# Scan products in a fixed order on TensorE, each step in one run between whole projection tiles, and tanh for the convolution's gate

## The chip, the core and the metric

The kernel runs on one core of a Trainium2 chip. The metric is the time of one execution on the device in microseconds (us); the time of the kernel before is the median of three runs. A core has TensorE (matrix products; PE in the profile, with its weight loads as PEld), VectorE (DVE), ScalarE (ACT), GpSimd (POOL), SyncE (SP, which here issues the DMAs) and 16 DMA engines. PSUM is the memory into which TensorE writes and from which VectorE and ScalarE read. Each engine works through its own list of instructions in order and waits on semaphores where a result of another is needed.

## The reference, cut to what matters

One layer of a hybrid block over 512 latent tokens of width 1024, with 256 context tokens ahead whose final scan state starts the scan of the latent ones. One input projection feeds a convolution branch (A) and a bidirectional scan (B), in 8 groups of 4 heads; then come gates, an output projection and an MLP. All is float32.

```python
h = modulate(rmsnorm(x, norm1_w), mod[0], mod[1]); proj = h @ w_in
# A: the gated input and a depthwise convolution of width 31 along grid rows of 64
glu = proj[..., COL_GLU:COL_GATE]
u = glu[..., :CONV_DIM] * jax.nn.sigmoid(glu[..., CONV_DIM:])
u = dwconv(u.reshape(rows, 64, CONV_DIM), conv_dw_w, conv_dw_b)
u_conv = silu(layernorm(u)) @ w_conv_out + b_conv_out
# B: for x, B and C a centred convolution of width 5 and SiLU, then, in each direction, by chunks of 128:
cum = jnp.cumsum(dt * a)
cb = jnp.einsum('bcqgn,bckgn->bcgqk', cs_, bs)
y_diag = jnp.einsum('bcgrqk,bckgrp->bcqgrp', cb[:, :, :, None] * decay, xdt)
states = jnp.einsum('bcqgn,bcqgr,bcqgrp->bcgrpn', bs, decay_to_end, xdt)
h_in = scan over the chunks of  h * chunk_decay + states      # from the context's final state
y_off = jnp.einsum('bcqgn,bcgrpn,bcqgr->bcqgrp', cs_, h_in, jnp.exp(cum))
y = y_f + flip(y_b) + ssm_d * xs
y = rmsnorm(y * silu(z), ssm_norm_w);  u_ssd = y @ w_ssm_out
x = x + mod[2] * ((g_conv * u_conv + g_ssd * u_ssd) @ w_o)      # g: sigmoid gates from proj
x = x + mod[5] * sq_relu_mlp(modulate(rmsnorm(x, norm2_w), ...))
```

## The kernel before

Channels lie on the 128 partitions and tokens in the free dimension. The input projection is cut into tiles of 128 output columns. For each, `load_w` (L99 to L107) brings the 512 KB weight tile by a DMA of SP's, ScalarE casts it to its high part `whi` (L105) and VectorE takes the difference, the low part `wlo` (L106). `gemm` (L109 to L116) then makes the product in three passes, `whi` by the input's high part (L114), `whi` by its low part (L115) and `wlo` by the high part (L116): 8 slices by 3, so 24 matmuls of 512 columns for a whole tile. The tiles of B and of the two x tiles (X0, X1) have 24 more of 256 columns for the context. Two weight tiles are held at a time (`raw`, `whi` and `wlo` have two buffers each), and the products go to three PSUM buffers `ps`.

A group's projection (`proj`, L415) gives six tiles: B, C, X0, X1 (`xbc`, L377) and the gates Z0, Z1. Those of B, C and x leave PSUM by `taps5` (L367 to L375), the convolution of width 5: one ScalarE instruction (L370) and four of VectorE (L374), then SiLU on ScalarE (L384). Those of Z leave by a SiLU (L430).

A group's scan (`ssd`, L437) has these steps, named here as in the change:

- **c**: B by C for the four chunks (`cps`, L442), masked on VectorE (`cbm`, L447), and B turned by TensorE (`bps`, L454) and copied by ScalarE (`Bk`, L455).
- **x**: x turned by TensorE (`xps`, L465), multiplied by VectorE with what reaches the chunk's end (`xw`, L470) and copied by ScalarE (`xt`, L477).
- **s**: the states' products (`sps`, L485) and their running sum on VectorE (`hst`, L491 to L498).
- **y0, y1**: the outputs of two heads each. A DMA (L507) brings the running sums of one head and direction (`cfb`). ScalarE makes the decays (four Relu, L510, and one Exp, L512), VectorE multiplies by `cbm` (L513), ScalarE (L517) and VectorE (L520) mix the two directions, and GpSimd or VectorE multiplies C by the decays (`Cd`, L523). TensorE adds 16 products of the states and `Cd` (L536) and 8 of x and the mix (L532) in one PSUM tile `yps`. VectorE adds D·x (L540), multiplies by Z (L541), and a DMA writes the tile (L542).

Branch A runs beside the scan. `glu` (L551) makes two projection tiles, takes the sigmoid of the one on ScalarE (L557) and multiplies with the other on VectorE (L562). `taps` (L565) is the convolution of width 31: one ScalarE instruction (L569) and 30 of VectorE (L575) for a tile of 128 channels.

The main loop (L585 to L593) traces `ssd(g)`, then `proj(g + 1)`, then, for the first five groups, a tile of branch A. The order on each engine is not that of the text: a scheduler picks the ready instruction of the best priority, and `later(n)` moves priorities (weights 300 earlier, evictions of projections 400 earlier, `glu` 90 later, `taps` 650 later). The order is fixed when the kernel is built. So matmuls of the scan stand among those of the projection tiles, wherever the scheduler took their inputs to be ready. After the scan come the other three tiles of branch A, the gates, branch A's LayerNorm, the two branch projections, the output projection and the MLP.

Of the kernel before, what the change touches and what calls it, by code (L numbers as in the profile page):

```python
# [26 lines left out]
# columns of the packed per-channel vectors  # L27
# [8 lines left out]
# order of the input projection's 128-column tiles  # L36
# [6 lines left out]
# the groups beside which the first tiles of the convolution module run  # L43
GLU_AT = (0, 1, 2, 3, 4)
# [12 lines left out]
def build(tc, xT, ctxT, cond, crow, wada1, wada2, vecs, hv, cst, w_in, w_co, w_so, w_o, w_1, w_2, outT):  # L57
    nc = tc.nc
    with ExitStack() as es:
# [49 lines left out]
        def gemm(ps, w, rhs, start=True, stop=True, t0=0, t1=None, k0=0, k1=KT):  # L109
# [3 lines left out]
            for k in range(k0, k1):  # L113
                nc.tensor.matmul(ps, lhsT=whi[:, k, :], rhs=rhi[:, k, t0:t1], start=start and k == 0, stop=False)  # L114
                nc.tensor.matmul(ps, lhsT=whi[:, k, :], rhs=rlo[:, k, t0:t1], start=False, stop=False)  # L115
                nc.tensor.matmul(ps, lhsT=wlo[:, k, :], rhs=rhi[:, k, t0:t1], start=False, stop=stop and k == KT - 1)  # L116
# [13 lines left out]
        def rsqrt_mean(ps, n, cnt, r=None):  # L130
            """1/sqrt(sum/cnt + EPS) of a sum broadcast over the partitions"""
# [18 lines left out]
        def rsqrt_rows(parts, n, cnt, pool, out=None):  # L150
            """the same of the sum of several tiles, found token by token and then spread over the partitions"""
# [40 lines left out]
        with tc.tile_pool(name="st", bufs=1) as st:  # L192
# [31 lines left out]
            # products of nothing: the tensor engine's clock halves when it idles  # L224
# [83 lines left out]
            # softplus: max(v, 0) + log1p(u), u = exp(-|v|), log1p(u) = 2 atanh(u / (2 + u))  # L308
# [13 lines left out]
            # running sums within the chunks and within the context, backward ones from the end  # L322
# [22 lines left out]
            # step s: chunk s forward, chunk 3 - s backward  # L345
# [41 lines left out]
        def xbc_first():  # L387
            """the first group's, all of x's part before ctx's"""
# [162 lines left out]
        def glu(t, pool, tag):  # L551
# [4 lines left out]
            with later(-EVICT_GLU):  # L556
                nc.scalar.activation(sg, pb, AF.Sigmoid)  # L557
# [319 lines left out]
```

## Time and profile before

| | us |
|---|---|
| three runs | 1263.03, 1266.08, 1270.63 |
| median | 1266.08 |
| profiled execution, span | 1264.2 |
| VectorE's first multiplication of step x (L470) of groups 0, 1, 2, 6, 7 | 104.1, 162.8, 235.2, 520.6, 577.3 |
| end of the scan's outputs | 621.6 |

The profile is of one execution; its times count from the start of its span. The median lies 1.9 us above the span. Step x is used as a mark below: "from x of group 1 to x of group 2" is the stretch between VectorE's first multiplication of step x (L470) in the one and in the other. A group row gives an instruction's line, engine, operation and tiles, how many there are, their busy time, the mean in ns of one, and then the engine's idle time just before them with what ended it. A timeline row gives start, duration and instruction, and `x8` where eight in a row were put together. The scan's float32 products are two records each in the trace; its turnings by TensorE (`bps`, `xps`) and the projections' matmuls (fp32r) are one.

### The profile page before, as it was taken

What the parts mean: (1) busy time and instruction counts of PE and PEld (TensorE: products, weight loads), DVE (VectorE), ACT (ScalarE), POOL (GpSimd) and SP (SyncE); (2) the same over time, 40 slices, a digit from 0 to 9 for tenths busy, and PEclk for the clock granted to TensorE, in tenths of its full rate; (3) what the DMA queues carried; (4) which work ended last, traced back from release to release, by engine and by line L of the source; (5) the groups of instructions that cost most, each with busy time, mean ns of one, the idle gap of its engine ahead of it and who ended that gap; (6) DMA issues with size and microseconds to landing.
All of it is one profiled execution on the core that took longest, in us unless ns stands there. A gap on an engine that the chain in (4) does not pass through costs nothing.

```text
span 1264.2 us, 17493 instructions
## 1 busy us (share of the span) xinstructions
PE 1220.7 (97%) x6665; PEld 995.6 (79%) x6665; DVE 953.7 (75%) x1567; ACT 667.4 (53%) x1124; POOL 108.9 (9%) x74
## 2 busy tenths in 40 slices
PE   6998999999999899999999999999999999999997
PEld 3786778777787778787888877778998888888886
DVE  6797689999999999998999798885843343443444
ACT  4557888686776748868453452134431331331442
POOL 0001222121020302124000000000000000000000
PEclk8999999999999999999999999999999999999999
DMA  9424363343342424333363357964222333233332
GB/s 363 142 67 133 137 198 128 120 146 106 121 159 93 158 83 147 112 134 117 109 193 126 119 188 258 305 196 153 62 65 86 100 100 92 92 100 101 96 104 67
DMA packets 56260, 169.96 MB, mean 134 GB/s; under 512 B 6640, under 2 KB 9584, under 8 KB 56048
## 3 DMA queue, kind: packets, MB, share of 16 engines
q1 hardware_dynamic: 56176, 168.85, 41.0%
q8 instruction: 52, 0.85, 0.3%
q14 instruction: 32, 0.26, 0.1%
HBM read 162.27 MB, written 6.55 MB: 134 GB/s over the span
## 4 chain that ended last, share of the span: by engine, by line
PE 65%; DVE 20%; DMA 8%; issue 3%; ACT 3%; SPq 0%; POOL 0%; DVEq 0%; ACTq 0%; POOLq 0%
PE ps L114 20%; PE ps L115 19%; PE ps L116 19%; DVE conv L575 5%; DVE wlo L106 3%; DVE Xt L374 3%; DMA aw<-in_wada_dram 2%; DMA cfb<-s_cf 2%; PE yps L536 2%; PE yps L532 2%; PE sps L485 1%; DMA yr<-s_y 1%; DVE aw L675 1%; DMA raw<-in_w_dram 1%; ACT whi L105 1%
## 5 line engine op out<-in xcount | busy, mean ns | idle before, releaser
L105 ACT CAST whi<-raw 128x1024 fp32r<-128x1024 f32 x163 | 170.9, 1049 | 320.6 <-PE ps L115 291.5
L106 DVE TENSOR_TENSOR wlo<-raw,whi 128x1024 fp32r<-128x1024 f32 x163 | 203.8, 1251 | 84.3 <-ACT whi L105 76.1
L114 PE MATMUL ps<-hh,whi 128*128 128x512 f32 x632 | 258.0, 408 | 2.3 <-DVE Xt L374 2.1
L116 PE MATMUL ps<-hh,wlo 128*128 128x512 f32 x632 | 255.4, 404 | 2.3 <-DVE wlo L106 2.2
L115 PE MATMUL ps<-hl,whi 128*128 128x512 f32 x632 | 256.7, 406 | 0.0
L575 DVE SCALAR_TENSOR_TENSOR conv<-sg,V,conv 128x480 f32<-128x480 f32 (+14 forms) x240 | 173.3, 740 | 2.6 <-ACT conv L569 1.1
L114 PEld LDWEIGHTS ps<-hh,whi 128*128 128x128 f32 x632 | 119.4, 189 | 30.8 <-issue 7.2
L116 PEld LDWEIGHTS ps<-hh,wlo 128*128 128x128 f32 x632 | 119.4, 189 | 30.7 <-DVE wlo L106 4.7
L115 PEld LDWEIGHTS ps<-hl,whi 128*128 128x128 f32 x632 | 119.6, 189 | 26.5 <-issue 3.7
L711 DVE SCALAR_TENSOR_TENSOR x<-ps,mod,x 128x512 f32<-128x512 f32 (+1 forms) x48 | 31.7, 660 | 100.1 <-PE ps L116 100.1
L510 ACT ACTIVATE e<-cfb,cfT 128x128 f32<-128x128 f32 x256 | 83.9, 391 | 36.8 <-PE yps L532 17.5
L523 POOL TENSOR_TENSOR Cd<-Ct,cfb 128x512 f32<-128x512 f32 x48 | 72.6, 1518 | 313.0 <-DMA cfb<-s_cf 250.3
L116 PE MATMUL ps<-h2h,wlo 128*128 128x512 f32 (+1 forms) x240 | 89.8, 375 | 0.0
L115 PE MATMUL ps<-h2l,whi 128*128 128x512 f32 (+1 forms) x240 | 89.8, 375 | 0.0
L114 PE MATMUL ps<-h2h,whi 128*128 128x512 f32 (+1 forms) x240 | 89.4, 375 | 0.0
L115 PE MATMUL ps<-gl,whi 128*128 128x512 f32 x224 | 88.4, 395 | 0.0
L114 PE MATMUL ps<-gh,whi 128*128 128x512 f32 x224 | 88.2, 394 | 0.0
L116 PE MATMUL ps<-gh,wlo 128*128 128x512 f32 x224 | 87.9, 392 | 0.0
L374 DVE SCALAR_TENSOR_TENSOR Xt<-ps,V,Xt 128x255 f32<-128x255 f32 (+3 forms) x128 | 74.2, 605 | 3.9 <-ACT Xt L370 3.6
L114 PE MATMUL ps<-hc,whi 128*128 128x256 f32 x184 | 52.5, 285 | 3.1 <-DVE Xt L374 3.1
L115 PE MATMUL ps<-hc,whi 128*128 128x256 f32 x184 | 52.4, 285 | 0.0
L116 PE MATMUL ps<-hc,wlo 128*128 128x256 f32 x184 | 52.1, 283 | 0.0
(259 smaller groups left out, 2417.5 us busy)
## 6 DMA issues: line engine op xcount, KB each, us to landing
raw<-in_w_in_dram SPq DMA_DIRECT2D x81, 512.0 KB, 3.6
cfb<-s_cf SPq DMA_DIRECT2D x64, 512.0 KB, 4.4
raw<-in_w_dram SPq DMA_DIRECT2D x64, 512.0 KB, 3.5
aw<-in_wada_dram SPq DMA_DIRECT2D x64, 256.0 KB, 4.3
ablk<-in_wada_dram SPq DMA_DIRECT2D x16, 512.0 KB, 8.6
raw<-in_w_so_dram SPq DMA_DIRECT2D x16, 512.0 KB, 3.7
s_y<-yt SPq DMA_DIRECT2D x16, 256.0 KB, 2.2
yr<-s_y SPq DMA_DIRECT2D x16, 256.0 KB, 3.6
```

Of the source, the lines that this page charges most:

```text
L105: nc.scalar.copy(hi, raw)
L106: nc.vector.tensor_tensor(lo, raw, hi, ALU.subtract)
L114: nc.tensor.matmul(ps, lhsT=whi[:, k, :], rhs=rhi[:, k, t0:t1], start=start and k == 0, stop=False)
L115: nc.tensor.matmul(ps, lhsT=whi[:, k, :], rhs=rlo[:, k, t0:t1], start=False, stop=False)
L116: nc.tensor.matmul(ps, lhsT=wlo[:, k, :], rhs=rhi[:, k, t0:t1], start=False, stop=stop and k == KT - 1)
L374: nc.vector.scalar_tensor_tensor(o[:, lo:hi], ps[:, lo + d:hi + d], vcol(V_SCW + 5 * ch + j), o[:, lo:hi], ALU.mult, ALU.add)
L510: nc.scalar.activation(ch(e, c), cb_[:, 0, c * P:(c + 1) * P], AF.Relu, bias=cfT[:, c, hd:hd + 1], scale=-1.0)
L523: (nc.vector if (d, r) in DECAYS_V else nc.gpsimd).tensor_tensor(Cd, Ct, cb_[:, 1, :], ALU.mult)
L532: nc.tensor.matmul(o, lhsT=xt[:, c, hr, :], rhs=ch(Ms[r], c), start=False, stop=True, skip_group_check=True)
L536: nc.tensor.matmul(o, lhsT=hst[:, s, k, hr * 64:hr * 64 + 64], rhs=ch(Cs[k][r], c), start=k == 0 and c == 0, stop=False, skip_group_check= ...
L575: nc.vector.scalar_tensor_tensor(o[:, :, lo:hi], u[:, :, lo + d:hi + d], wv(j), o[:, :, lo:hi], ALU.mult, ALU.add)
L711: nc.vector.scalar_tensor_tensor(x1[:, j, a:b], ps[:, a:b], mod[:, gcol + j, 0:1], x1[:, j, a:b], ALU.mult, ALU.add)
```

## The change

The input projection, the scan and branch A are cut into steps, and a string lists the steps of a round in the order in which TensorE is to do them. While `in_order` is set (the rounds 0 to 6), `pe` keeps each matmul in program order on TensorE; the other engines' instructions are still placed by priorities. A round holds steps s, y0 and y1 of the current group, the projections B, C, X0, X1, Z0, Z1 of the next, steps c and x of the next, and the two projection tiles of branch A (Gb, Ga). In round 0 the two tiles of branch A come first, ahead of steps c and x of group 0 (`c0`, `x0`). Round 7 has no order to keep.

The sigmoid of the gate is written as tanh of half the argument, plus one, with the taps' weights halved once by a VectorE instruction on 248 columns. This holds for all eight tiles of branch A. The diff also takes out the comments.

```diff
+STEPS0 = 'Gb Ga c0 B x0 C s X0 y0 X1 y1 c Z0 Z1 x'
+STEPS = 'B s Gb C X0 y0 Ga X1 y1 c Z0 Z1 x'
+NGLU = 5
...
-                nc.tensor.matmul(ps, lhsT=whi[:, k, :], rhs=rhi[:, k, t0:t1], start=start and k == 0, stop=False)
+                pe(nc.tensor.matmul(ps, lhsT=whi[:, k, :], rhs=rhi[:, k, t0:t1], start=start and k == 0, stop=False))
...
+        in_order = [False]
+
+        def pe(ins):
+
+            if in_order[0]:
+                tc.keep_in_program_order(ins)
...
+        nc.vector.tensor_scalar(V[:, V_DWW:], V[:, V_DWW:], 0.5, None, ALU.mult)
...
+        def proj(q, part):
+
+            g = q["g"]
+            s = W_GRP + 6 * g
+            j = int(part[1:] or 0)
+            if part == "B":
+                q[part] = xbc(s, 16 + g, True, "Bt")
+            elif part == "C":
+                q[part] = xbc(s + 1, 24 + g, False, "Ct")
+            elif part[0] == "X":
+                q[part] = xbc(s + 2 + j, 2 * g + j, True, "Xt")
...
-                nc.scalar.activation(sg, pb, AF.Sigmoid)
+                nc.scalar.activation(sg, pb, AF.Tanh, scale=0.5)
+            return t, sg
+
+        def glu_a(t, sg):
             wa = load_w(w_in[W_GLU + 2 * t + 1])
             pa = ps_big()
             gemm(pa, wa, rh)
             with later(-EVICT_GLU):
-                nc.vector.tensor_tensor(sg, sg, pa, ALU.mult)
+                nc.vector.scalar_tensor_tensor(sg, sg, 1.0, pa, ALU.add, ALU.mult)
             return t, sg
...
         for g in range(G):
-            ssd(g, *cur)
-            if g + 1 < G:
-                cur = proj(g + 1)
-            if g in GLU_AT:
-                with later(GLU_LATER):
-                    q = glu(GLU_AT.index(g), spool, "sg")
-                with later(TAPS_LATER):
-                    taps(*q)
-        late = list(range(len(GLU_AT), KT))
+            nxt = group(g + 1)
+            glu_q = None
+            for part in STEPS0.split() if g == 0 else STEPS.split():
+                in_order[0] = g < G - 1
+                if part[0] in "BCXZ":
+                    if g + 1 < G:
+                        proj(nxt, part)
...
+                elif part == "s":
+                    ssd_s(cur)
+                elif part[0] == "y":
+                    ssd_y(cur, int(part[1]))
+                elif part == "Gb":
+                    if begun_glu < NGLU:
+                        glu_q = glu_b(begun_glu, spool, "sg")
+                        begun_glu += 1
+                elif glu_q is not None:
+                    glu_q = glu_a(*glu_q)
+                    with later(TAPS_LATER):
+                        taps(*glu_q)
+                    glu_q = None
+            cur = nxt
+        in_order[0] = False
```

The functions `ssd_c`, `ssd_x`, `ssd_s` and `ssd_y` are the four parts of `ssd` as it was. What the diff doesn't show is how the built order differs. TensorE turns from other products to output products (`yps`) 66 times before and 19 times now. ScalarE's table loads go from 74 to 83: those at the decays' Exp from 28 to 35, those at the SiLU of x, B and C from 19 to 26, those at Z's SiLU from 7 to 9; the seven at the sigmoid of the gate are gone. The taps of branch A (L575) lie differently between the marks of step x: before, 0 up to group 0's and 0 from there to group 1's, 18 from group 1's to group 2's, 114 from group 2's to group 6's, 19 from group 6's to group 7's; now 9, 14, 11, 114 and 2. There is one tile of branch A less between group 2's and group 6's step x (three where there were four), and one more ahead of group 0's.

TensorE before, at the last output products of y1 of group 2 (`yps_2399`); `ps_2604` is a projection tile of the next round:

```order
L532 MATMUL yps_2399<-e_2402,xt_2259 64x128
L115 MATMUL ps_2604<-hl_77,whi_2599 128x512
L116 MATMUL ps_2604<-hh_76,wlo_2600 128x512
L114 MATMUL ps_2604<-hh_76,whi_2599 128x512
L115 MATMUL ps_2604<-hl_77,whi_2599 128x512
L116 MATMUL ps_2604<-hh_76,wlo_2600 128x512
L114 MATMUL ps_2604<-hh_76,whi_2599 128x512
L532 MATMUL yps_2399<-e_2432,xt_2259 64x128
L532 MATMUL yps_2399<-e_2402,xt_2259 64x128
L115 MATMUL ps_2604<-hl_77,whi_2599 128x512
```

TensorE now, at the end of the same output tile (`yps_2739`), with step c of group 3 (`cps_2831`, `bps_2841`, `bps_2847`) and the tile Z0 of group 3 (`ps_2857`) behind it:

```order
L568 MATMUL yps_2739<-e_2772,xt_2260 64x128
L568 MATMUL yps_2739<-e_2742,xt_2260 64x128
L568 MATMUL yps_2739<-e_2772,xt_2260 64x128
L469 MATMUL cps_2831<-Ct_2415,Bt_2292 128x128 x4
L481 MATMUL bps_2841<-C_73,Bt_2292 128x128 x4
L481 MATMUL bps_2847<-C_73,Bt_2292 128x128 x2
L119 MATMUL ps_2857<-hh_76,whi_2853 128x512
L120 MATMUL ps_2857<-hl_77,whi_2853 128x512
```

The output products stood among those of a projection tile in several pieces; now the 24 of them stand together, then step c, then a whole tile.

VectorE before, just ahead of the addition that ends y1 of group 2 (L540): the last mixes `e_2432` stand among the taps of the next group's C (`Ct_2565`).

```order
L374 SCALAR_TENSOR_TENSOR Ct_2565<-ps_2566,V_72,Ct_2565 128x511
L520 SCALAR_TENSOR_TENSOR e_2432<-e_2447,dtT_574,e_2432 128x128
L374 SCALAR_TENSOR_TENSOR Ct_2565<-ps_2566,V_72,Ct_2565 128x510
L520 SCALAR_TENSOR_TENSOR e_2432<-e_2447,dtT_574,e_2432 128x128 x2
L575 SCALAR_TENSOR_TENSOR conv_716<-sg_2173,V_72,conv_716 128x8x49
L540 SCALAR_TENSOR_TENSOR yt_2484<-Xt_2014,V_72,yps_2399 128x512
```

VectorE now, at the same place (L576 is that addition): the last two mixes `e_2772` stand behind the taps of both parts of X1 of the next group (`ps_2678` of the latent tokens, `ps_2708` of the context) and a weight tile's low part.

```order
L385 SCALAR_TENSOR_TENSOR Xt_2677<-ps_2678,V_72,Xt_2677 128x511
L385 SCALAR_TENSOR_TENSOR Xt_2677<-ps_2708,V_72,Xt_2677 128x254
L385 SCALAR_TENSOR_TENSOR Xt_2677<-ps_2678,V_72,Xt_2677 128x510
L385 SCALAR_TENSOR_TENSOR Xt_2677<-ps_2708,V_72,Xt_2677 128x255
L111 TENSOR_TENSOR wlo_2887<-raw_2884,whi_2886 128x1024
L385 SCALAR_TENSOR_TENSOR Xt_2677<-ps_2708,V_72,Xt_2677 128x255
L556 SCALAR_TENSOR_TENSOR e_2772<-e_2787,dtT_574,e_2772 128x128
L385 SCALAR_TENSOR_TENSOR Xt_2677<-ps_2708,V_72,Xt_2677 128x254
L556 SCALAR_TENSOR_TENSOR e_2772<-e_2787,dtT_574,e_2772 128x128
L559 TENSOR_TENSOR Cd_3216<-Ct_2415,cfb_3203 128x512
L576 SCALAR_TENSOR_TENSOR yt_2824<-Xt_2020,V_72,yps_2739 128x512
```

The mixes that y1 needs moved from among the taps of C to behind those of X1, and X1 is the tile that TensorE does just ahead of y1. No tap of the long convolution stands between them and the addition now.

More of the change, by code (lines that the diff above doesn't have):

```diff
@@ L551, in glu, with ssd_y @@
-        def glu(t, pool, tag):
+            q["hst"] = hst
+        def ssd_y(q, j):
+            g, Ct, cbm, xt, hst, X, Z = q["g"], q["C"], q["cb"], q["xt"], q["hst"], q[f"X{j}"], q[f"Z{j}"]
+            yps = py.tile([P, T], F32, name="yps", tag="py")
+            Ms, Cs = [], ([], [])
+            for r in range(2):
+                for d in range(2):
+                    hd = d * HEADS + 4 * g + 2 * j + r
+                    cb_ = spool.tile([P, 2, T], F32, name="cfb", tag="cfb", bufs=3)
+                    nc.sync.dma_start(cb_, s_cf[hd].unsqueeze(0).broadcast_to([P, 2, T]))
+                    e = (spool if d else tp).tile([P, T], F32, name="e", tag="e" if d else "M", bufs=2 if d else 3)
+                    for c in range(NCH):
+                        nc.scalar.activation(
+                            ch(e, c), cb_[:, 0, c * P:(c + 1) * P], AF.Relu, bias=cfT[:, c, hd:hd + 1], scale=-1.0)
+                    nc.scalar.activation(e, e, AF.Exp, scale=-1.0)
+                    nc.vector.tensor_tensor(e, e, cbm[d].rearrange("p c q -> p (c q)"), ALU.mult)
+                    if d == 0:
+                        M = e
+                        for c in range(NCH):
+                            nc.scalar.activation(ch(M, c), ch(M, c), AF.Copy, scale=dtT[:, c, hd:hd + 1])
+                    else:
+                        for c in range(NCH):
+                            nc.vector.scalar_tensor_tensor(
+                                ch(M, c), ch(e, c), dtT[:, c, hd:hd + 1], ch(M, c), ALU.mult, ALU.add)
+                    Cd = (spool if d else tp).tile([P, T], F32, name="Cd", tag="Cd", bufs=4 if d else 3)
+                    (nc.vector if (d, r) in DECAYS_V else nc.gpsimd).tensor_tensor(Cd, Ct, cb_[:, 1, :], ALU.mult)
+                    Cs[d].append(Cd)
+                Ms.append(M)
+            for k in range(3):
+                for c in range(NCH):
+                    for r in range(2):
+                        o = yps[64 * r:64 * r + 64, c * P:(c + 1) * P]
+                        hr = 2 * j + r
+                        if k == 2:
+                            pe(nc.tensor.matmul(o, lhsT=xt[:, c, hr, :], rhs=ch(Ms[r], c),
+                                             start=False, stop=True, skip_group_check=True))
+                        else:
+                            s = 3 - c if k else c
+                            pe(nc.tensor.matmul(o, lhsT=hst[:, s, k, hr * 64:hr * 64 + 64], rhs=ch(Cs[k][r], c),
+                                             start=k == 0 and c == 0, stop=False, skip_group_check=True))
+            t = 2 * g + j
+            yt = tp.tile([P, T], F32, name="yt", tag="yt", bufs=2)
+            nc.vector.scalar_tensor_tensor(yt, X[:, :T], vcol(V_D + t), yps, ALU.mult, ALU.add)
+            nc.vector.tensor_tensor(yt, yt, Z, ALU.mult)
+            nc.sync.dma_start(s_y[t], yt)
+            if t == 0:
+                nc.scalar.activation(yacc, yt, AF.Square)
+            else:
+                y2 = spool.tile([P, T], F32, name="ysq", tag="ysq", bufs=1)
+                nc.scalar.activation(y2, yt, AF.Square)
+                nc.gpsimd.tensor_tensor(yacc, yacc, y2, ALU.add)
@@ L552, in glu, with glu_b @@
+        def glu_b(t, pool, tag):
             wb = load_w(w_in[W_GLU + 2 * t])
@@ L583, in build @@
         conv = first_xbc[0]
[L584 removed]
+        cur = group(0)
+        proj(cur, "Z0")
+        proj(cur, "Z1")
+        begun_glu = 0
         for g in range(G):
[L586 to L594 removed]
+            nxt = group(g + 1)
[5 more added lines that the diff above has]
+                        proj(nxt, part)
+                elif part in ("c", "x"):
+                    if g + 1 < G:
+                        (ssd_c if part == "c" else ssd_x)(nxt)
+                elif part in ("c0", "x0"):
+                    (ssd_c if part == "c0" else ssd_x)(cur)
+                elif part == "s":
[13 more added lines that the diff above has]
+        in_order[0] = False
+        late = list(range(NGLU, KT))
         inner.close()
```

98 lines of the change are left out of this document (26 added, 72 removed).

## The prediction

> **What bounds the kernel now.** I read the page first, then a table of stretches, cut at the marks of step x.
>
> ```profile
> span 1264.2 us, 17493 instructions
> PE 1220.7 (97%) x6665; PEld 995.6 (79%) x6665; DVE 953.7 (75%) x1567; ACT 667.4 (53%) x1124; POOL 108.9 (9%) x74
> ```
>
> By the page TensorE is the bound. The table of stretches says otherwise for part of the program.
>
> ```profile
> core 0: us, PE busy (x) PEld busy (x) DVE busy (x) ACT busy (x) POOL busy (x), PEclk, DMA share, GB/s
> 77.30:104.13 26.83, 25.27 (x138) 21.19 (x137) 25.59 (x51) 14.44 (x27) 0.00 (x0) 1.00 0.31 89
> 104.13:162.84 58.71, 53.91 (x314) 41.83 (x313) 41.40 (x71) 47.51 (x93) 11.03 (x9) 0.97 0.49 152
> 162.84:235.20 72.36, 70.55 (x418) 57.29 (x417) 64.25 (x100) 59.28 (x119) 19.46 (x13) 1.00 0.51 169
> 235.20:520.60 285.40, 276.22 (x1620) 222.76 (x1619) 274.22 (x439) 206.19 (x379) 49.65 (x35) 0.99 0.38 124
> 520.60:577.30 56.70, 55.84 (x348) 45.33 (x347) 53.64 (x96) 39.46 (x73) 12.13 (x6) 1.00 0.32 108
> 577.30:621.60 44.30, 44.08 (x261) 34.94 (x259) 40.77 (x69) 30.00 (x62) 9.93 (x6) 1.00 0.40 134
> 621.60:1264.20 642.60, 629.93 (x3071) 526.46 (x3069) 396.10 (x634) 229.15 (x308) 6.53 (x3) 1.00 0.41 129
> ```
>
> The reader is to see the third and fourth columns of the row 235.20:520.60, which holds four groups: TensorE is busy 276.22 of 285.40 us and VectorE 274.22. Both are nearly full, and VectorE's list has only 11.2 us of idle time. What VectorE waits for there is short:
>
> ```profile
> DVE yt L540 <- PE yps L532: 5.6, 6, 1.5
> ```
>
> Half of its idle time (5.6 us) is the addition that ends y0 or y1, waiting for the last output products. Is TensorE really full there? A busy matmul may wait inside its record, so I count starts. The timeline of TensorE in group 2:
>
> ```profile
> 262.29 0.39 PE L114 MATMUL ps<-hh,whi 128*128 128x512 f32 x1
> ...
> 267.73 0.39 PE L114 MATMUL ps<-hh,whi 128*128 128x512 f32 x1
> 268.04 1.85 PE L536 MATMUL yps<-Cd,hst 128*64 128x128 f32 x29
> ...
> 271.20 0.39 PE L114 MATMUL ps<-hh,whi 128*128 128x512 f32 x1
> 271.52 0.44 PE L532 MATMUL yps<-e,xt 128*64 128x128 f32 x4
> 271.89 0.50 PE L115 MATMUL ps<-hl,whi 128*128 128x512 f32 x1
> 272.23 0.39 PE L116 MATMUL ps<-hh,wlo 128*128 128x512 f32 x1
> 272.46 0.40 PE L114 MATMUL ps<-hh,whi 128*128 128x512 f32 x1
> ```
>
> The first two rows are 24 records apart: 5.44 us, or 0.227 each and 5.45 for a whole tile. In the third row an output record takes about 0.055 (1.85 less the last one's tail, by 29). From 271.20 to 272.46 stand three projection matmuls (0.68) and four output records (0.22), 0.90 together, in 1.26 us. So a turn to output products and back costs about 0.35 us. The next rows price the 256-column matmuls and the scan's steps.
>
> ```profile
> 93.82 0.28 PE L114 MATMUL ps<-hc,whi 128*128 128x256 f32 x1
> ...
> 96.69 0.40 PE L114 MATMUL ps<-hh,whi 128*128 128x512 f32 x1
> 513.53 1.06 PE L442 MATMUL cps<-Ct,Bt 128*128 128x128 f32 x8
> 514.42 0.82 PE L454 MATMUL bps<-C,Bt 128*128 128x128 f32 x6
> 519.13 1.03 PE L465 MATMUL xps<-C,Xt 128*128 128x128 f32 x8
> 522.14 4.63 PE L485 MATMUL sps<-xw,Bk 128*128 128x256 f32 x20 [0.81 <-DVE xw L470]
> ```
>
> 24 context matmuls take 2.87 us, 0.12 each. Each burst less the last record's tail gives a group's small steps: c 0.9 and 0.65, x 1.3 (12 records), s 4.3, the outputs 96 records or 5.3: 12.5 us. So a group with a tile of branch A needs of TensorE 8 x 24 x 0.227 = 43.6, 72 x 0.12 = 8.6, 12.5 and, with two turns, 0.7: 65.4 us. Without that tile it is 54.5. Three with and one without make 250.7 for four groups, well below VectorE's 274.22. VectorE bounds groups 2 to 5, and TensorE is there only a little behind.
>
> **The change part by part.** The prices of VectorE's work:
>
> ```profile
> L106 DVE TENSOR_TENSOR wlo<-raw,whi 128x1024 fp32r<-128x1024 f32 x163 | 203.8, 1251 | 84.3 <-ACT whi L105 76.1 <-PE sum L147 4.4
> L575 DVE SCALAR_TENSOR_TENSOR conv<-sg,V,conv 128x480 f32<-128x480 f32 (+14 forms) x240 | 173.3, 740 | 2.6 <-ACT conv L569 1.1
> L374 DVE SCALAR_TENSOR_TENSOR Xt<-ps,V,Xt 128x255 f32<-128x255 f32 (+3 forms) x128 | 74.2, 605 | 3.9 <-ACT Xt L370 3.6
> L520 DVE SCALAR_TENSOR_TENSOR e<-e,dtT 128x128 f32<-128x128 f32 x128 | 42.6, 358 | 0.2
> L562 DVE TENSOR_TENSOR sg<-sg,ps 128x512 f32<-128x512 f32 x8 | 5.4, 679 | 0.3 <-PE ps L116 0.2
> L370 ACT ACTIVATE Xt<-ps,V 128x512 f32<-128x512 f32 (+1 forms) x32 | 21.2, 664 | 16.3 <-PE ps L116 16.1
> ```
>
> *Fewer turns.* 66 turns become 19: 47 x 0.35 = 16.5 us of TensorE's time. This is the gain on offer; it comes through only where TensorE, not VectorE, ends the stretch.
>
> *The wait at y1.* TensorE now may not leave y1 before it is done. By the order, the last mixes of y1 stand behind the evictions of X1's two parts and a `wlo`, and X1 is the tile just ahead. From X1's last matmul to the last mix pass one ScalarE eviction (0.66), some five taps (5 x 0.605), a `wlo` (1.25) and two mixes (2 x 0.358): 5.6 us. y1's own first 32 records cover 1.9 to 2.1 of it. I take 3.5 us a group. What is queued behind y1 on TensorE is steps c, Z0, Z1 and x; who waits for it is the addition L540 and then the addition's buffers. It is nothing at the least (if VectorE runs the mixes earlier than the rows suggest) and 5.6 at most.
>
> *To x of group 1 (77.30 to 162.84).* One tile of branch A (two projection tiles, 10.9 us of TensorE) and 9 + 14 taps move in. VectorE was busy 25.59 + 41.40 = 67.0 of 85.5 us. It gains 23 x 0.74 = 17.0, two `wlo` and one `sg` (3.2): 87.2 us. TensorE, 79.2 busy, gains 10.9 and loses about 12 turns (4.2): 85.9. Both fit just so. With 2 us of idle time on VectorE: 89.2, **+3.7**. Bounds: +1.7 (no idle) to +10.9 (the two tiles in full).
>
> *From x of group 1 to x of group 2.* Seven taps less leave VectorE with 59.1, so TensorE ends it: 65.4 + 3.5 + 0.5 of other waits = 69.4 against 72.36, **-3.0**. Bounds: -7.0 (no wait) to 0.
>
> *From x of group 2 to x of group 6.* 114 taps before and 114 now. One tile of branch A less takes two `wlo` and one `sg`, 3.2 us, from VectorE: 271.0. TensorE needs 250.7 and 4 x 3.5 of waits, 264.7, so VectorE bounds it still. Idle time: the 5.6 at L540 went with output products in pieces, and I let it go; the other 5.6 stays. 276.6 against 285.40, **-8.8**. Bounds: -14.4 (no idle time) to +5.2 (rival C).
>
> *From x of group 6 to x of group 7.* Only 2 taps remain where 19 were, so VectorE has about 41 and TensorE ends it: 54.5 + 3.5 + 0.5 = 58.5 against 56.70, **+1.8**. Bounds: -2.2 (no wait) to +4.6 (both outputs wait).
>
> *The rest.* From 577.30 on the same work is left, and the taps still open are as many. The last group has no fixed order. 0, within 1.5 us for the scan's end and 3 for the tail.
>
> *Tanh, and ScalarE's loads.* The halving of the weights is one small VectorE instruction early; the new product adds one to `sg` on its way. Both I put at nothing. The table loads go from 74 to 83:
>
> ```profile
> L512 ACT ACT_TABLE_LOAD x28 | 35.9, 1283 | 0.5
> L557 ACT ACT_TABLE_LOAD x7 | 9.0, 1283 | 0.1
> ```
>
> Nine more are 9 x 1.283 = 11.5 us of ScalarE, spread over 460 us in which it is busy at most 82% of a stretch (59.28 of 72.36). What hides them is that idle time; if it were gone the cost would be the 11.5. Is a load all that a switch costs? ScalarE's timeline:
>
> ```profile
> 152.74 1.28 ACT L512 ACT_TABLE_LOAD   x1
> 154.04 0.63 ACT L512 ACTIVATE e<-e 128x512 f32<-128x512 f32 x1
> ```
>
> The next instruction starts 0.02 us after the load's end, so I take 1.28. The Trainium skill, page "ScalarE: Activation LUTs", section "What ACT_TABLE_LOAD costs", adds a drain of about 1380 ns to each switch, some 2.66 us in all. By that price nine more loads would be an estimate of 24 us of ScalarE, and the forecast would stand higher by up to that; this trace shows no such gap behind the load, and the measurement decides.
>
> *Sum.* +3.7 - 3.0 - 8.8 + 1.8 = -6.3 on the profiled 1264.2, or 1257.9. The median lies 1.9 above that execution: **1259.8 us**. With the smaller bounds (no more than 5 us at L540 and the mixes, the first stretch between +1.7 and +7) this case's own range is 1251 to 1268.
>
> **The rivals.**
>
> *B: the turns' saving comes through in full.* The mixes run early, y1 waits for nothing, and VectorE idles nowhere in groups 2 to 5. For: VectorE's idle time there is only 11.2 us, half of it due to the pieces. Against: the order of the mixes. +1.7 - 7.0 - 14.4 - 2.2 = -21.9: 1244.2.
>
> *C: the fixed order is a chain (slower).* While TensorE waits at y1, its projection tiles stop, and VectorE, once the mixes are done, has no evictions and stands idle as long. Then 3.5 us a group lie on the path though VectorE has more work: 271.0 + 5.6 + 4 x 3.5 = 290.6, +5.2. The first stretch takes +7.3 (midway between 3.7 and 10.9), the second 0, the fourth +4.6: +17.1, 1283.2. It decides if VectorE idles more than about 3.6 us a group between x of groups 2 and 6, where 1.4 makes my forecast and 2.8 was before. For: three PSUM buffers and two weight buffers let VectorE run at most a few tiles away from TensorE, and before, other matmuls could go ahead of a late input. Against: taps of branch A, ready at any time, fill VectorE's idle time.
>
> *D: ScalarE's table loads decide.* Its work is late at the Exp ahead of the mixes, so that each of the nine loads lies on the path: 1259.8 + 11.5 = 1271.3. Against: ScalarE's busy shares above. The Trainium skill's page "ScalarE: Activation LUTs" speaks for this case, with its higher price of a switch.
>
> *E: nothing is gained.* The turns' saving turns into other idle time: VectorE saves its 3.2 and no more, +3.7 + 0 - 3.2 + 1.8 = +2.3: 1268.4.
>
> **How the numbers follow.** Forecast 0.44, B 0.17, C 0.24, D 0.05, E 0.10. A measurement of this kernel can tell about 0.5%, 6.3 us. Faster than 1259.8 are B and half of the forecast (0.40 with a little of E); within 0.5% the other half of it, E and half of D (0.33); slower C and the rest (0.27). The range runs from B's time to C's, 1244 to 1283, which leaves out half of each, 0.20.
>
> **What would show it.** In the changed kernel's table of stretches: VectorE busy about 271 between x of groups 2 and 6 with 4 to 8 us idle; TensorE waiting at y1 for a mix (L556) some 3 us a group; next to nothing at the final addition for output products. If VectorE idles over 14 us there, C is right; if TensorE never waits at y1, B. A stretch up to x of group 1 longer than 92 us, or a tail that differs from 642.6 by over 3 us, would show the sum wrong in its first or last term.

## The result, and the profile after

The changed kernel takes 1275.35 us (median of six runs, 1274.45 to 1276.71) against 1265.12 for the kernel before in six runs: a ratio of 1.0085, 95% interval 1.0063 to 1.0108. It is slower, where 1259.8 and faster was forecast; the range (1244 to 1283) holds it. The profiled execution has a span of 1273.5 us, 9.3 more than before.

The table of stretches of the changed kernel, cut at the same marks (the last but one ends, as before, at the sum of y's squares):

```profile
77.30:124.93 47.63, 40.21 (x208) 33.90 (x206) 36.65 (x64) 25.57 (x55) 5.80 (x4) 0.96 0.45 143
124.93:178.95 54.02, 47.36 (x291) 41.03 (x292) 53.04 (x90) 47.27 (x92) 10.50 (x7) 0.87 0.45 152
178.95:245.15 66.20, 66.15 (x410) 56.88 (x409) 58.19 (x99) 57.23 (x106) 14.94 (x9) 1.00 0.40 132
245.15:526.93 281.78, 263.43 (x1578) 224.13 (x1577) 273.42 (x430) 202.87 (x369) 57.01 (x35) 0.96 0.37 123
526.93:587.02 60.09, 54.84 (x347) 47.18 (x346) 50.17 (x81) 50.22 (x94) 12.09 (x9) 0.97 0.36 118
587.02:633.34 46.32, 45.45 (x269) 36.31 (x268) 41.08 (x67) 22.80 (x47) 4.72 (x3) 1.00 0.38 117
633.34:1273.50 640.16, 629.33 (x3071) 527.00 (x3069) 393.54 (x629) 229.52 (x308) 8.26 (x3) 0.99 0.41 130
```

Two columns matter. The last but two is TensorE's granted clock: 0.87, 0.96 and 0.97 in stretches that had 0.97, 0.99 and 1.00. And in the fourth row VectorE is busy 273.42 of 281.78 us, so it does bound groups 2 to 5.

| from ... to ... | before | forecast | after |
|---|---|---|---|
| 77.30 to x of group 1 | 85.54 | +3.7 | 101.65 (+16.1) |
| to x of group 2 | 72.36 | -3.0 | 66.20 (-6.2) |
| to x of group 6 | 285.40 | -8.8 | 281.78 (-3.6) |
| to x of group 7 | 56.70 | +1.8 | 60.09 (+3.4) |
| to the sum of squares | 44.30 | 0 | 46.32 (+2.0) |
| tail | 642.60 | 0 | 640.16 (-2.4) |

The loss is in the first row, and the gain of the third is less than half of what was forecast. What TensorE waits for in the scan of the changed kernel (us in total, times, longest):

```profile
PE yps L568 <- DVE e L556: 18.4, 8, 5.2
PE sps L518 <- DVE xw L499: 8.4, 1, 8.4
PE sps L518 <- ACT hst L524: 6.9, 5, 3.2
PE ps L121 <- DVE wlo L111: 4.3, 2, 3.2
```

The first is the wait at y0 and y1 for a mix. In the kernel before, where other matmuls could go ahead, the same pair cost 0.6 us:

```profile
PE yps L532 <- DVE e L520: 0.6, 2, 0.4
```

The longest of the eight are at y1 of groups 0, 2, 5 and 6: 5.2, 4.4, 3.2 and 2.8 us. The second row of the waits above is the first block, group 0. Its rows, from the chain (first row), then VectorE's timeline and TensorE's:

```profile
100.02 12.58 DMA cfb<-s_cf
```
```profile
103.39 4.06 DVE L614 SCALAR_TENSOR_TENSOR conv<-sg,V,conv 128x392 f32<-128x392 f32 x6
114.66 0.69 DVE L549 TENSOR_TENSOR e<-e,cbm 128x512 f32<-128x512 f32 x1 [7.22 <-ACT e L548]
...
124.93 3.13 DVE L499 TENSOR_TENSOR xw<-xps,wgT 128x512 f32<-128x512 f32 x6
```
```profile
126.36 7.20 PE L518 MATMUL sps<-xw,Bk 128*128 128x256 f32 x20 [8.44 <-DVE xw L499]
```

The DMA of the first running sums lands at 112.6 us. The first decay product (L549) waits for it, 7.22 us, and step x's multiplications (L499) stand behind that product on VectorE's list, though their data is there. Behind the product come 9.6 us of other work that also stands ahead of them: three taps of branch A, the eight of B, one product of C by the decays and a `wlo`. TensorE idles 8.44 us.

The place that the order showed, y1 of group 2, by the timelines of VectorE and GpSimd, and then of TensorE:

```profile
296.81 0.34 DVE L556 SCALAR_TENSOR_TENSOR e<-e,dtT 128x128 f32<-128x128 f32 x1
297.07 2.17 DVE L385 SCALAR_TENSOR_TENSOR Xt<-ps,V,Xt 128x511 f32<-128x511 f32 x4
297.70 2.52 POOL L559 TENSOR_TENSOR Cd<-Ct,cfb 128x512 f32<-128x512 f32 x2 [1.62 <-DMA cfb<-s_cf]
299.17 2.14 DVE L111 TENSOR_TENSOR wlo<-raw,whi 128x1024 fp32r<-128x1024 f32 x1
301.23 0.47 DVE L385 SCALAR_TENSOR_TENSOR Xt<-ps,V,Xt 128x255 f32<-128x255 f32 x1
301.62 0.34 DVE L556 SCALAR_TENSOR_TENSOR e<-e,dtT 128x128 f32<-128x128 f32 x1
```
```profile
302.01 1.34 PE L568 MATMUL yps<-e,xt 128*64 128x128 f32 x6 [4.37 <-DVE e L556]
303.28 2.08 PE L469 MATMUL cps<-Ct,Bt 128*128 128x128 f32 x8
```

The mix at 301.62 comes 4.8 us after the one at 296.81; between them stand the taps of X1 and the `wlo`, as forecast. But the `wlo` took 2.14 us, not 1.25: GpSimd was multiplying C by the decays (297.70 to 300.22). And behind the wait the eight records of step c take 2.08 us where they took 1.06 before. The table of 2-us stretches around it says why:

```profile
296.00:298.00 2.00, 1.16 (x16) 0.65 (x12) 2.00 (x5) 1.34 (x2) 0.38 (x2) 1.00 0.70 264
298.00:300.00 2.00, 0.00 (x0) 0.00 (x0) 2.00 (x4) 0.00 (x0) 2.00 (x2) 0.74 0.03 12
300.00:302.00 2.00, 0.00 (x0) 0.00 (x0) 2.00 (x4) 0.00 (x0) 0.22 (x1) 0.50 0.00 0
302.00:304.00 2.00, 1.99 (x9) 1.31 (x10) 1.82 (x4) 1.23 (x2) 0.00 (x0) 0.50 0.80 199
304.00:306.00 2.00, 2.00 (x12) 2.00 (x11) 0.74 (x3) 1.30 (x2) 0.00 (x0) 0.55 0.20 72
306.00:308.00 2.00, 2.00 (x12) 1.66 (x11) 2.00 (x5) 1.89 (x6) 0.41 (x1) 1.00 0.23 86
```

The clock is halved within the wait and comes back at about 306. From 302.01 to 306.36 TensorE did work of 2.1 us at full clock, so the drop cost some 2 us more. By such tables of the whole scan the clock falls seven times in the changed kernel (at waits of 2.75 to 8.44 us) and twice in the one before (at 3.15 and 2.12 us). Half of the time in which TensorE was busy at half clock is what it lost: 1.7 to 2.9 us a drop, 16.4 us in all, against 3.4 before.

VectorE's mixes as a group, in the changed kernel:

```profile
L556 DVE SCALAR_TENSOR_TENSOR e<-e,dtT 128x128 f32<-128x128 f32 x128 | 55.8, 468 | 3.7 <-ACT e L553 3.3
```

They took 42.6 us before (L520). 106 of the 128 take 0.34 us; the 22 that ran while GpSimd was at work take 1.07 on average. In all VectorE is busy 512.56 us from 77.30 to the sum of squares, with 499.85 before, for the same instructions but four. That is 12.7 us more in a scan that grew by 11.7.

### The profile page after: what moved, and what is told of

Read it like the earlier page. It is cut to its first block, busy times and chain, and to the rows that moved or that the text cites. A ratio compares the mean times of both kernels' runs of the same rounds, so it can differ in the third digit from the quotient of the medians.

```text
span 1273.5 us, 17506 instructions
## 1 busy us (share of the span) xinstructions
PE 1211.3 (95%) x6665; PEld 1011.7 (79%) x6665; DVE 964.4 (76%) x1568; ACT 678.3 (53%) x1133; POOL 113.5 (9%) x74
## 4 chain that ended last, share of the span: by engine, by line
PE 58%; DVE 24%; DMA 7%; ACT 7%; issue 3%; SPq 0%; DVEq 0%; ACTq 0%
PE ps L119 18%; PE ps L120 18%; PE ps L121 18%; DVE conv L614 5%; DVE wlo L111 4%; DVE Xt L385 2%; DVE e L556 2%; DMA cfb<-s_cf 2%; DMA aw<-in_wada_dram 2%; DVE e L549 2%; PE sps L518 1%; DVE xw L499 1%; ACT e L546 1%; DMA yr<-s_y 1%; DMA raw<-in_w_dram 1%
## 5 line engine op out<-in xcount | busy, mean ns | idle before, releaser
L119 PE MATMUL ps<-hh,whi 128*128 128x512 f32 x632 | 253.3, 401 | 0.6 <-DVE Bt L385 0.4
L121 PE MATMUL ps<-hh,wlo 128*128 128x512 f32 x632 | 249.1, 394 | 4.6 <-DVE wlo L111 4.6
L120 PE MATMUL ps<-hl,whi 128*128 128x512 f32 x632 | 248.5, 393 | 0.0
L614 DVE SCALAR_TENSOR_TENSOR conv<-sg,V,conv 128x392 f32<-128x392 f32 (+14 forms) x240 | 168.3, 719 | 1.6
L546 ACT ACTIVATE e<-cfb,cfT 128x128 f32<-128x128 f32 x256 | 84.1, 393 | 42.2 <-DMA cfb<-s_cf 16.4
L119 PE MATMUL ps<-h2h,whi 128*128 128x512 f32 (+1 forms) x240 | 89.4, 375 | 0.0
L385 DVE SCALAR_TENSOR_TENSOR Xt<-ps,V,Xt 128x510 f32<-128x510 f32 (+3 forms) x128 | 74.9, 608 | 8.9 <-ACT Xt L381 8.5
L556 DVE SCALAR_TENSOR_TENSOR e<-e,dtT 128x128 f32<-128x128 f32 x128 | 55.8, 468 | 3.7 <-ACT e L553 3.3
L549 DVE TENSOR_TENSOR e<-e,cbm 128x512 f32<-128x512 f32 x64 | 50.7, 803 | 9.0 <-ACT e L548 9.0
L518 PE MATMUL sps<-xw,Bk 128*128 128x256 f32 x160 | 41.3, 411 | 15.4 <-DVE xw L499 8.4
```

Source lines behind the costliest of these rows:

```text
L119: pe(nc.tensor.matmul(ps, lhsT=whi[:, k, :], rhs=rhi[:, k, t0:t1], start=start and k == 0, stop=False))
L120: pe(nc.tensor.matmul(ps, lhsT=whi[:, k, :], rhs=rlo[:, k, t0:t1], start=False, stop=False))
L121: pe(nc.tensor.matmul(ps, lhsT=wlo[:, k, :], rhs=rhi[:, k, t0:t1], start=False, stop=stop and k == KT - 1))
L385: nc.vector.scalar_tensor_tensor(o[:, lo:hi], ps[:, lo + d:hi + d], vcol(V_SCW + 5 * ch + j), o[:, lo:hi], ALU.mult, ALU.add)
L518: pe(nc.tensor.matmul(ps[:, d * 256:(d + 1) * 256], lhsT=ch(Bk, c), rhs=xw[d][:, wi[d](c)].rearrange("p h e -> p (h e)"), start=i == 0, st ...
L546: nc.scalar.activation(ch(e, c), cb_[:, 0, c * P:(c + 1) * P], AF.Relu, bias=cfT[:, c, hd:hd + 1], scale=-1.0)
```

## The experiments

Each was timed beside the kernel before (1263 to 1265 us in these runs); times are medians, the ratio is to the kernel before. Changed kernel: 1275.35.

**1. Step x of group 0 ahead of B.**

```diff
-STEPS0 = 'Gb Ga c0 B x0 C s X0 y0 X1 y1 c Z0 Z1 x'
+STEPS0 = 'Gb Ga c0 x0 B C s X0 y0 X1 y1 c Z0 Z1 x'
```

> Step x of group 0 stands ahead of tile B in round 0, so VectorE's six multiplications of step x (L499) stand ahead of the first decay product (L549), which waits for ScalarE's Exp and so for the DMA of the running sums. Theory W (waits on VectorE's list, each long one followed by a low clock): TensorE's idle time of 8.4 us at the states' products of group 0 goes, and the clock drop behind it (2.7 us): 1275.35 - 11 = 1264. Theory V (VectorE is the bound, TensorE's waits are only its shadow): VectorE still waits 7.2 us for that Exp, so the end moves by 3 us at most: 1272 to 1275.

Measured: 1272.26 us, 1.0051 (1.0025 to 1.0076). Step x of group 0 started at 104.5 us instead of 124.9, but the states' products then waited 6.6 us for the copy of the first state on ScalarE, where the Relu of the decays, waiting for the same DMA, stands ahead. The wait had moved from VectorE's list to ScalarE's. The time is the one that theory V named, but by this other wait.

**2. Z0 between X1 and y1.**

```diff
-STEPS = 'B s Gb C X0 y0 Ga X1 y1 c Z0 Z1 x'
+STEPS = 'B s Gb C X0 y0 Ga X1 Z0 y1 c Z1 x'
```

and the same in STEPS0.

> The tile Z0 stands between X1 and y1 in every round, 5.45 us more for the mixes that y1's last products need. Theory W: the waits of the output products for a mix (18.4 us in eight) fall below 5 us, and the four clock drops at them go (2.7 us each): up to 24 us less, 1251 to 1257. Theory V: between step x of groups 2 and 6 VectorE is busy 273.4 of 281.8 us, so no more than 8 us can come from there, and some 8 from the two waits outside it: 1260 to 1268. Theory O (any fixed order is a chain): the wait goes to the next step, and the time stays within 4 us of 1275.

Measured: 1255.53 us, 0.9931 (0.9908 to 0.9954): 20 us below the changed kernel, and faster than the one before. TensorE's waits, and the stretch between step x of groups 2 and 6:

```profile
PE sps L518 <- ACT hst L524: 11.3, 4, 3.6
PE sps L518 <- DVE xw L499: 8.4, 2, 6.5
PE yps L568 <- DVE e L556: 2.1, 3, 1.6
```
```profile
238.03:509.03 271.00, 256.22 (x1573) 218.81 (x1572) 267.45 (x426) 203.54 (x377) 55.44 (x35) 0.98 0.38 129
```

y1's wait is down to 2.1 us; 271.00 against 281.78, with VectorE idle 3.6 us in place of 8.4. The first block still waits (6.5 us). Theory O falls, and theory V's cap of 8 us for that stretch too: 10.8 came, since VectorE's busy time fell as well (267.45).

**3. The changed steps, without the kept order on TensorE.**

```diff
-            if in_order[0]:
+            if False:
                 tc.keep_in_program_order(ins)
```

> The steps are traced in the changed kernel's order, but TensorE's matmuls are placed by priorities as before (36 turns to output products). Theory W: ready matmuls of projection tiles stand in front of late output products again, so the idle time goes: near the kernel before, 1262 to 1268. Rival S (not the fixed order but the sequence of steps, computed a round ahead, is at fault): it stays at 1273 to 1277.

Measured: 1254.81 us, 0.9917 (0.9886 to 0.9948), 20.5 below the changed kernel. So the sequence of steps, computed a round ahead, was good, and the loss comes with keeping each step whole on TensorE.

**4. The kernel before, with tanh alone.** The sigmoid, the product and the halved weights as in the change, nothing else.

> The kernel before with tanh in place of the sigmoid, the product with one added and the weights halved; its order comes out with 45 turns and 61 table loads (66 and 74 before). Theory W: the tanh is free, and 21 turns less give TensorE about 6 us, of which part comes through: 1260 to 1266. Rival S2 (the tanh costs): 1268 or more.

Measured: 1262.91 us, 0.9989 (0.9967 to 1.0011). Tanh, with 21 turns and 13 table loads less, brought at most 4 us and cost nothing that can be measured.

**5 and 9. Products of nothing at the waits.** The fifth put 30 ahead of the states of group 0 and 12 ahead of y1 of four groups; the ninth only the latter.

```diff
+            if j == 1 and g in (0, 2, 5, 6):
+                for _ in range(12):
+                    pe(nc.tensor.matmul(yps, lhsT=rh[0][:, 0, :P], rhs=rh[0][:, 0, :], start=True, stop=True))
```

> The changed kernel with products of nothing on TensorE in front of places where it waited over 2.7 us: 30 (6.8 us) ahead of the states' products of group 0, and 12 (2.7 us) ahead of y1 of groups 0, 2, 5 and 6. The waits for VectorE stay, only TensorE doesn't idle so long, so the clock should not fall there. Theory K (the low clock behind a wait is a cost of its own, 2.7 us each): up to five drops go, 4 to 14 us: 1261 to 1271. Theory W0 (only the waits cost): 1275 or more, since a filler longer than its wait adds time.

> As the fifth experiment, without the 30 products of nothing at group 0's states (there they stood behind the wait and not in it, since they needed a free PSUM buffer): only the 12 (2.7 us) ahead of y1 of groups 0, 2, 5 and 6. The waits for the mixes stay on VectorE's side; TensorE idles less than 3 us at them. Theory K (a low clock behind a wait is a cost of its own): the drops at these four go, 4 x 2.7 us, 1262 to 1268. Theory W0 (only the waits cost): 1274 to 1279.

Measured: 1271.49 us, 1.0054 (1.0026 to 1.0083), and 1263.00 us, 0.9998 (0.9978 to 1.0017). 48 useless products, 2.7 us in each of four groups, made the kernel 12 us faster. The profile of the ninth is of its slowest execution (1268.14 us, 7.5 below that of the changed kernel). TensorE's waits for a mix there are

```profile
PE yps L571 <- DVE e L556: 4.3, 4, 2.4
```

in place of 18.4 us, but 10.8 us of useless products fill most of the difference, so these places are only some 3 us shorter. The clock falls five times, one of them at y1 (group 0's), and costs 9.2 us in place of 16.4. The 30 products of the fifth stood behind group 0's wait and cost their own 7 us. The order on VectorE came out different too (its mixes take 50.1 us in place of 55.8), so how much of the 12 us is the clock's alone isn't shown. The forecast by which only the waits cost (W0) did not come.

**6. Both, the first and the second.**

> Z0 ahead of y1 as in the second experiment, and step x of group 0 ahead of B as in the first. If the two gains add (20 and 3 us): 1251 to 1254. If the first block's wait only moves to ScalarE's list (the copy of the first state, as the first experiment's trace showed, 6.6 us): 1254 to 1258.

Measured: 1255.88 us, 0.9939 (0.9916 to 0.9963): no better than the second alone. The wait for the copy of the first state on ScalarE is there again, 6.0 us, as the second alternative had it.

**7 and 8. Both kernels with few taps.**

```diff
-                if d == 0:
+                if d == 0 or (t < 5 and abs(d) > 3):
                     continue
```

> The changed kernel with 24 of the 30 VectorE taps left out in the first five tiles of branch A (part of the computation is left out): 120 x 0.72 = 86 us of VectorE's work gone from the scan. Theory V (VectorE bounds groups 2 to 5): the stretch from x of group 2 to x of group 6 falls from 281.8 to TensorE's own 250 to 262, and the time by 25 us or more, to 1235 to 1250. Theory O (TensorE's waits in the fixed order are a chain that VectorE's load does not make): 1265 or more.

> The kernel before with the same taps left out. With VectorE's load gone, the turns that the change saves must show: theory V expects the kernel before to be slower than the changed one by 8 to 16 us when both have few taps (1250 to 1260 here); theory O expects it to be as fast or faster.

Measured: 1252.99 us, 0.9910 (0.9883 to 0.9937), for the changed kernel and 1248.97, 0.9885 (0.9848 to 0.9923), for the one before. The stretch of four groups, changed kernel, then the one before:

```profile
241.00:508.14 267.14, 252.56 (x1560) 217.13 (x1560) 216.58 (x334) 207.38 (x374) 49.49 (x35) 0.99 0.37 127
```
```profile
234.36:504.41 270.05, 265.77 (x1626) 224.72 (x1624) 217.66 (x349) 196.11 (x372) 53.67 (x36) 1.00 0.41 133
```

(Both profiled executions are the slowest of their kernel.) 57 us less of VectorE's work shorten the stretch by 14.6 and 15.4 us only: VectorE bounds it, and TensorE with its waits is 15 us behind, about where the prediction put it (264.7 against 267.14). The expected lead of the changed kernel didn't come: its waits (8.8 us at the output products, 19 at the states) are there without VectorE's load too, so theory O holds for that part. Theory V's time for the changed kernel (1235 to 1250) was missed by 3 us.

**10 and 14. The mixes earlier on VectorE's list**, in all groups and in groups 1 to 7; TensorE's order stays. `MIX` is 600; the fourteenth has `-MIX if g else 0` in its place.

```diff
+                    with later(-MIX):
                         nc.vector.tensor_tensor(e, e, cbm[d].rearrange("p c q -> p (c q)"), ALU.mult)
...
+                      with later(-MIX):
                         for c in range(NCH):
```

> TensorE's order is that of the changed kernel but for the last group; VectorE's decay products and mixes (L549, L556) get a priority 600 earlier, so the mixes of y1 stand ahead of the evictions of X1 instead of behind them. Theory W (the loss is the mixes' place on VectorE's list): the 18.4 us of waits at the output products and the clock drops behind them go as with Z0 ahead of y1: 1252 to 1260. Theory O (the fixed order on TensorE, y1 straight behind X1, is at fault): 1270 or more.

> The mixes' priority of the tenth run in groups 1 to 7 alone, so the first block stays as in the changed kernel. Theory W: the tenth run's gain behind the first block stays (16 us between step x of groups 2 and 6), and its loss in the first block (8 us of wait more, and the clock) goes: 1252 to 1260. If y1's waits were not what cost: 1268 or more.

Measured: 1265.68 us, 1.0013 (0.9997 to 1.0030), and 1269.27 us, 1.0049 (1.0032 to 1.0065): 10 and 6 us below the changed kernel, less than expected; the fourteenth lies where it was put in case y1's waits were not what cost. In the tenth, y1's waits are gone and others stand in their place:

```profile
PE sps L519 <- DVE xw L500: 23.7, 3, 16.5
PE sps L519 <- ACT hst L525: 13.3, 6, 4.9
PE ps L122 <- DVE wlo L112: 1.9, 2, 1.6
PE yps L571 <- DVE e L559: 0.5, 1, 0.5
```

The decay products now stand ahead of step x more often, 16.5 us in the first block. In the fourteenth the four groups take 265.54 us, 16 less than in the changed kernel, but the two stretches up to x of group 2 stay as long, and the next to x of group 7 is 5 us longer (step s waits 3.7 and 6.1 us). So the four groups gain, and the stretches around them lose part of it again.

**11, 12 and 15. Step s in two runs.** The first state's product is one step, the other three another, with tile C between (round 0: X0), beside Z0 ahead of y1. The twelfth adds the tenth's priorities, the fifteenth the mended first block of the thirteenth.

```diff
+STEPS0 = 'Gb Ga c0 B x0 C s X0 s2 y0 X1 Z0 y1 c Z1 x'
+STEPS = 'B s C s2 Gb X0 y0 Ga X1 Z0 y1 c Z1 x'
...
```

> Z0 ahead of y1, and step s in two runs with tile C (in round 0 tile X0) between them, so that the first state's copy on ScalarE, for which the states' products waited 11.3 us in four places (L518 for L524), has a tile's time. If that wait and its clock drops (three at most, 2.7 us each) are on the path: 1240 to 1249. If VectorE (busy 267.45 of 271.0 us between step x of groups 2 and 6) covers them: 1251 to 1256.

> The last one with the mixes' priority of the tenth as well. If y1's waits are gone with Z0 ahead of it already, nothing more: within 3 us of the eleventh.

> Z0 ahead of y1, step s in two runs, and the first block mended as in the thirteenth. If the first block's wait (5.9 us in the eleventh, and 3.4 us of clock) is on the path there: 1243 to 1248. If it is given back by the work behind it: 1250 to 1254.

Measured: 1251.89 us, 0.9919 (0.9895 to 0.9943), 23 us below the changed kernel, but by its interval no better than the second and third experiments: as its second alternative had it, the wait for the copy was covered. The twelfth takes 1275.11 us, 1.0103 (1.0079 to 1.0128), 23 us above the eleventh where 3 at most were expected, with 16.2 us of wait in the first block; and the fifteenth 1289.94 us, 1.0216 (1.0193 to 1.0238), far above its forecast, with the wait that the thirteenth shows below.

**13. The first block alone.** Steps c0, x0, s, B, C, with the copies of x and of the state and the Relu of group 0 kept in program order on ScalarE.

```diff
-STEPS0 = 'Gb Ga c0 B x0 C s X0 y0 X1 y1 c Z0 Z1 x'
+STEPS0 = 'Gb Ga c0 x0 s B C X0 y0 X1 y1 c Z0 Z1 x'
...
-                        nc.scalar.activation(
-                            ch(e, c), cb_[:, 0, c * P:(c + 1) * P], AF.Relu, bias=cfT[:, c, hd:hd + 1], scale=-1.0)
+                        first(q)(nc.scalar.activation(
+                            ch(e, c), cb_[:, 0, c * P:(c + 1) * P], AF.Relu, bias=cfT[:, c, hd:hd + 1], scale=-1.0))
```

> Only the first block changed: in round 0 the steps stand as c0, x0, s, B, C, and on ScalarE the copies of x and of the first state are kept ahead of the decays' Relu of group 0, so neither VectorE's nor ScalarE's list makes the states wait for the running sums' DMA. If the first block (8.4 us of wait and a long time at half clock behind it) is on the path: 9 to 13 us below the changed kernel, 1262 to 1266. If the time is given back, as in the first experiment: 1269 to 1274.

Measured: 1305.42 us, 1.0322 (1.0283 to 1.0361). Step x started at 104.1 us, but the first Relu came only at 146.7, long after its DMA, and TensorE waited 22.7 us in two places for products of C by the decays. It mends one wait by a larger one, and tells nothing of the first block's price.

**16 and 17. No products of GpSimd's for y1**, in both kernels; TensorE takes C itself, so y1 lacks that factor of the decays.

```diff
+                    if j == 1 and (d, r) not in DECAYS_V:
+                        Cs[d].append(Ct)
+                    else:
...
```

> The changed kernel without GpSimd's products of C and the decays for y1 (24 of 48; TensorE takes C itself, so that factor is left out of y1). If GpSimd slows the mixes that y1 waits for: VectorE's mixes fall from 55.8 to about 49 us, y1's waits (18.4 us) by a third, and the time by 8 to 15 us: 1260 to 1267. If the slowing only fills time in which VectorE would idle: 1271 to 1276.

> The same left out of the kernel before, where 10 mixes were slowed and only to 0.56 us, but TensorE waits 6.2 us in three places for those products. If GpSimd costs the order before little: 1258 to 1265. If it costs it as much as the changed one: 1250 to 1257.

Measured: 1251.93 us, 0.9911 (0.9884 to 0.9938), and 1251.05 us, 0.9902 (0.9878 to 0.9926). Mixes of the sixteenth:

```profile
L556 DVE SCALAR_TENSOR_TENSOR e<-e,dtT 128x128 f32<-128x128 f32 x128 | 46.8, 396 | 0.3 <-ACT e L553 0.2
```

Leaving out these 24 products brings the changed kernel 23 us (22 by the ratios) and the one before 12 (1263.5 in these runs). Without them the two orders are equal. The changed kernel gained more than its forecast (1260 to 1267), and y1's waits fell less, from 18.4 to 14.8 us, so shorter waits at y1 alone don't make up the 23 us. The edit also takes waits for those products away and frees buffers. That the changed order pays some 10 us more for these products than the old one is shown; by which of these ways is not.

## Why the prediction was wrong

*The stage was read rightly.* VectorE bounds groups 2 to 5 with TensorE some 15 us behind (runs 7 and 8), so the 16.5 us of saved turns could not come through there in full. Tanh cost nothing that run 4 could measure. ScalarE's table loads, rival D, did not decide: there are 83 in the changed kernel, 85 in run 9 and 81 in run 16, which are 12 and 23 us faster. The wait at y1 was named at its place and for its cause, and 4.4 us in group 2 is within its bounds; but it came in full at four of the seven groups only (0, 2, 5 and 6), not at each. (A small slip: rival C's +4.6 for two waits from x of group 6 on is +5.3 by its own terms, 54.5 + 7.0 + 0.5 - 56.70.)

*The step that failed is "To x of group 1"*, +3.7 with a bound of +10.9, measured +16.1; a stretch above 92 us was its own sign of being wrong, and 101.65 came. It counted the work that moved in and gave VectorE 2 us of idle time. The work was about as counted (VectorE busy 89.7 us for 87.2, TensorE 87.6 for 85.9), but VectorE idled 12.0 us and TensorE 14.1. The sum put TensorE's waits there at nothing, though y1 of group 0 stands behind X1 as in every other round; its own 3.5 us would have made TensorE's side 89.4, no more than the 89.2 that it took, so that alone didn't decide. Above all it did not look at what stands in whose list while the first running sums come by DMA. Group 0's decay product stands ahead of step x in VectorE's order. The waits there are 8.4 us at the states and 5.2 at y1, each with a clock drop behind it that cost 2.7 and 2.6 us. Z0 ahead of y1 alone brings x of group 1 from 179.0 to 168.1 us (166.5 by the forecast), with the first block's wait in place. What the first block costs by itself stays open: run 1 and run 6 moved it, and runs 10, 12, 13 and 15 made it or its neighbours worse.

*Two terms were missing from every wait.* First, the clock: behind seven waits of 2.75 us and more it was halved, and 2.3 us more were lost on average. 3.5 us a group were put on the path as 3.5. Run 9 speaks for it: useless products ahead of four waits bring 12 us. Second, the price of VectorE's instructions was taken from the rows of before (0.358 for a mix, 1.25 for a `wlo`), but the change put mixes beside GpSimd's products. That is 13 us more for the mixes. Between x of groups 2 and 6 they take 26.7 us (60 of them) where 64 took 21.8 before, and VectorE was busy 273.42 us there and not 271.0. Runs 16 and 17 show that the 24 products of GpSimd's for y1 are worth about the whole difference between the kernels. Slower mixes can make longer waits, and these make the clock fall, so the gains can't be added: the useless products, Z0 ahead of y1, the free order and GpSimd's products, each alone, bring 12 to 23 us, of a loss of 10.

*Rival C had the right sign and not the right mechanism.* VectorE did not idle more: 8.4 us between x of groups 2 and 6, 2.1 a group, below its 3.6. It was busy longer. TensorE's idle time in the scan rose from 18.4 to 38.6 us. With 13 us more of clock drops that is more than the 16.5 us that the turns were to save. So the time lies in the forecast's range by luck: the range reaches up to rival C's time, and C's chain through an idle VectorE did not come.

*What the change got right* shows in run 3: the same steps placed freely are 0.83% faster than the kernel before (0.9917).

## What to carry to other kernels

Keeping steps whole on an engine takes away the other work that hid its waits; before doing so, read on the lists of the other engines what stands ahead of each input, and leave a whole tile of unrelated work (here Z0, 5.45 us) between the producer's last input and the step. A wait of TensorE's of 2 us or more can cost more than itself, so look at the granted clock behind it and price both. An instruction that is moved beside another engine's work doesn't keep the duration of its old row.

## What the runs showed of the hardware

*The clock.* By stretches of 0.1 us, the granted clock at y1 of group 2 went to 0.50 at 298.98 us, 1.3 us after TensorE had stopped at 297.64, and came back at 305.80, 3.8 us after work began again. In the changed kernel's scan each low time lasts 3.41, 6.83 or 10.24 us, and their starts lie whole numbers of 3.413 us apart: 37.55 us from 121.48 to 159.03 (11), 139.95 on to 298.98 (41), 88.74 on to 387.72 (26). Cut into such periods from 77 to 620 us, the traces of the 19 kernels here show what comes before a drop. In the period just ahead of each of the 76 drops TensorE was busy 1.76 us or less of the 3.41 by the profile; in the 2759 periods behind which the clock stayed whole it was busy 1.41 us or more. So in these traces a period with TensorE idle for about half of it halves the clock at its end. The Trainium skill, page "TensorE: Matmul & The Clock Gate", section "What's actually happening", has the clock halved after at least one idle window of about 3.4 us and restored after a busy one, on windows that run freely. The traces agree on the length and on the free running, but no whole idle window was needed here: a wait of 2.12 us stands ahead of a drop in the kernel before. In the second experiment one of 3.33 us left the clock whole. It lies across two periods, in which TensorE was still busy 1.46 and 2.04 us:

```profile
318.00:320.00 2.00, 0.00 (x0) 1.00 0.02 6
320.00:322.00 2.00, 0.85 (x5) 1.00 0.27 104
```

*VectorE beside GpSimd.* A mix takes 0.34 us alone and up to 1.39 beside a GpSimd product of about 1.3 us. The Trainium skill, page "SBUF — State Buffer", section "Who interferes with whom", says that a VectorE instruction with two inputs in SBUF (the on-chip memory that holds the tiles) contends with a GpSimd instruction that reads SBUF, that their shared port is an exclusive lock, and that the order of issue decides which of them blocks. The trace agrees: the mixes and decay products, with two such inputs, reach 1.39 and 1.79 us, while the taps of X1 (one input from PSUM) stay at 0.75 at the most. This rule spoke against the change, and the prediction did not weigh it.
